# A hybrid decoder layer on one core: the down projection's first right blocks on GpSimd's DMA queue, its last chunk's steps in another order, and the closing squares of the rows ahead of their scalings

## The chip, the cores and the metric

The kernel runs on one core of a Trainium2 chip. Its engines work side by side, each with its own instruction stream: TensorE (PE in the profile, its weight loads PEld) multiplies, VectorE (DVE) does elementwise work on two operands, ScalarE (ACT) does elementwise functions of one operand and row sums of them, GpSimd (POOL) here only issues DMA transfers, among them those that add to what the target holds, and SyncE (SP) only issues plain transfers. An engine waits for another through semaphores, and what stands behind a waiting instruction on the same engine waits with it. The metric is the device time of one execution in microseconds (us), the median of several runs; lower is better.

## The reference

One decoder layer on x of 1024 tokens by 1024 channels, in fp32, cut to what matters here:

```python
h = rms_norm(x, g_mix)
z = h @ w_in + b_in
...                                   # a convolution branch and a recurrent branch, gated and merged
x = x + m @ w_o
h = rms_norm(x, g_mlp)
f = jnp.square(jax.nn.relu(h @ w_1))  # 1024 tokens x 4096
x = x + f @ w_2                       # the down projection: 4096 -> 1024
return rms_norm(x, g_final)
```

`rms_norm(y, g)` is `y * rsqrt(mean(y * y) + EPS) * g`, by rows (tokens). The change touches the last two lines: the down projection `f @ w_2` and the final norm.

## The kernel before

**Arithmetic.** Every fp32 operand of a product is split into a high part (rounded to the matmul's input type fp32r) and a low part, the remainder; high x high, low x high and high x low are summed. A high part is an ACT copy. The remainder is made in one of two ways: by a DVE subtraction (`low`, L1175), or by `split_dma` (L63): ACT writes the negated source as fp32r (L65), a DMA on GpSimd's queue adds the source to it (L66), and ACT writes the high part (L67).

**Down projection.** `f @ w_2` is done by a Winograd form of Strassen's scheme: tokens, inner dimension and output columns are halved, and seven products p = 1 to 7 take the place of eight. The inner dimension is cut into four chunks g = 0 to 3 (`NC_`), and a product has two halves kk in each; so a chunk has 14 steps m = 0 to 13, of 24 matmuls each. Steps run p = 1, 2, 6, 5, 7, 3, 4, in the last chunk 1, 2, 6, 5, 3, 7, 4. Within a step two halves of the tokens q2 = 0, 1 are two groups of 12 matmuls.

**Names in the trace.** `fd` is the DRAM buffer with f's blocks, written by `up_first` (from tiles `fa`, L1717) and `up_second` (from `fb`, L1709). `ar` and `br` are raw left blocks (from `fd`) and right blocks (from `w_2`), loaded by `d_load` (L1820). `s` and `t` are their sums and differences (`d_sum`, L1829; `t1`, `t3`, `t4`, `s3`, `s4` overwrite a raw block). `da_60h` and `da_60l` are the high and low left operand of p = 6, kk = 0 in any chunk, `db_...` the right one; the text writes `da3_60l` where the chunk matters. `d0a`, `d0b`, `d0e` are the PSUM units of chunk 0, each of 1024 columns, from a pool of four. `acc` are the four output quadrants in SBUF; `xb` are blocks of the residual that start or join them (`x_block`, L1975).

**What a step does.** `left_high` (L1867) makes the next step's left operand, `right` (L1875) the right operand of the step after that. `right` takes `split_dma` for p = 1 in chunk 0; for kk = 0 and for p = 2 and 5 in the other chunks; and the DVE subtraction otherwise. `down_mm` issues the matmuls, `down_add` (L1962) copies p = 1's result to the unit `b` (ACT, L1966), so that p = 2 can go on in unit `a`, and adds the other results to `acc` (DVE, L1970). `SUMS` and `LAST` say in which step each of the sums is made, `XADD` when a residual block is added.

**Entry.** The up projection runs before, in the same written order. Its last steps call `entry(k)`, k steps before the end: the loads of chunk 0 (all on SP's queue), and the first operands (`right(0, 1, 0)`, `left_high(0, 1, 0)`, `right(0, 1, 1)`). `DLOADS` lists the blocks by the step of the chunk before in which they are loaded for the other chunks; `DFIRST`, two more left blocks, follow in step 0 of their own chunk.

**End.** In the last chunk `FX` adds work to the steps: squares of finished rows with their row sums (`out_sq`), products with the final gain (`out_pre`), root and scaling of the first four row tiles (`out_root`, `out_scaled`), and operands of p = 4 and 7 by `by_dma`. The product p = 4 comes last and apart: `d_last` (L2032) puts unit `b` plus the accumulator into PSUM units `f`, and four groups of 12 matmuls add p = 4 to f0 to f3, one row tile of 128 tokens each. f0 and f1 are the halves of one PSUM unit; f2 and f3 have one each. `close(n)` (L2045) then finishes row tile 4 + n: square and row sum of `f` (ACT, L2050), root (ACT, L2051), reciprocal with a Newton step (DVE, L98 to L105), scaling of both column halves (DVE, L2056 and L2058; for the last two tiles ACT, L2055), and the transfer to the output.

**Order.** ACT, DVE and PE run in the order in which the code issues (`manual_schedule`); the order on SP's and POOL's queues is the scheduler's. Pools of SBUF tiles are rings: a load waits until the tile that had its place is no longer read. Tiles of one pool hold `fa`, `fb` and the operands `da`, `db`; another holds raw blocks, sums and the rows of the output. The last lines of the code before:

```python
d_group(du["f", 0], z, 4, 0, (0, 1), False, True)
d_last(1)
out_root(1)
out_sq(1, 1, 0)
out_scaled(1)
out_sq(1, 1, 1)
out_pre(1, 1, 1)
d_group(du["f", 1], z, 4, P, (0, 1), False, True)
close(0)
d_group(du["f", 2], z, 4, 2 * P, (0, 1), False, True)
close(1)
d_group(du["f", 3], z, 4, 3 * P, (0, 1), False, True)
close(2)
close(3)
```

Of the kernel before, what the change touches and what calls it, by code (L numbers as in the profile page):

```python
# [12 lines left out]
AF = mybir.ActivationFunctionType  # L13
ALU = mybir.AluOpType
# [3 lines left out]
D = 1024  # L18
# [6 lines left out]
EPS = 1e-6  # L25
# [5 lines left out]
def trunk_kernel(ctx: ExitStack, tc: tile.TileContext, x, xt_in, xt_eo, vecs, w_in, w_a_out, w_b_pl, w_b_sq,  # L31
                 w_rg, w_o, w_1, w_2, g_final, out):

    nc = tc.nc
# [19 lines left out]
    HALVES = (slice(0, HS), slice(HS, S))  # L54
# [729 lines left out]
    for i in range(2, NZ):  # L784
        n = zseq.index((i, 1))
# [18 lines left out]
    with tc.manual_schedule(engines=ENGINES):  # L804
        for s in range(3, NC1):
# [45 lines left out]
            for d in range(5):  # L851
                if s - d in EXP:
                    g = EXP[s - d]
# [6 lines left out]
                    t = 3 * g + d - (2 if g < 3 else 1)  # L860
# [119 lines left out]
    with tc.manual_schedule(engines=ENGINES):  # L980
# [72 lines left out]
        sb, yb_, fs = {}, {}, {}  # L1053
# [86 lines left out]
        for n in range(len(zseq) + 2):  # L1140
# [9 lines left out]
            if n + 3 < len(zseq):  # L1150
                i, p = zseq[n + 3]
# [26 lines left out]
    q, mean, vacc, rstd, nsum, nspl = {}, {}, {}, {}, {}, {}  # L1178
# [131 lines left out]
    m, sa, x1 = {}, {}, {}  # L1310
# [501 lines left out]
    NC_ = NP // KC  # L1812
# [7 lines left out]
    def d_load(g, *what):  # L1820
        for side, b, kk in what:
            n = 2 * g + kk
            ab[side, g, kk, b] = a = T(f"{side}r{n}_{b}")
            if side == "a":
                nc.sync.dma_start(v3(a), fd[2 * n:2 * n + 2, :, BLK[b], :].rearrange("k p c -> p k c"))
            else:
                nc.sync.dma_start(a, w_2[n, b // 10 - 1, b % 10 - 1])

    def d_sum(g, kk, name):  # L1829
        n = 2 * g + kk  # L1830
# [42 lines left out]
        split_dma(*d_pair(side, g, p, kk))  # L1873

    def right(g, p, kk):  # L1875
        if (p == 1 if g == 0 else not kk or p in (2, 5)):
            by_dma("b", g, p, kk)
            return lambda: None
        src, h, l = d_pair("b", g, p, kk)
        nc.scalar.activation(h, src, AF.Copy)  # L1880
        return lambda: low(l, src, h)
# [5 lines left out]
    DFIRST = ("a", 22, 1), ("a", 12, 1)  # L1887

    def entry(k):
        if k == 10:  # L1890
            for n in range(5, 9):
                d_load(0, *DLOADS[n])
        elif k == 7:
            d_load(0, *DLOADS[9])
        elif k == 6:
            d_load(0, *DLOADS[10], DLOADS[11][0])
        elif k == 5:
            d_load(0, DLOADS[11][1], *DLOADS[12])
            right(0, 1, 0)
        elif k == 4:  # L1900
            left_high(0, 1, 0)()
            d_load(0, *DLOADS[13])
        elif k == 3:
            right(0, 1, 1)

    ready = 4
    with tc.manual_schedule(engines={mybir.EngineType.Activation, mybir.EngineType.DVE,
                                     mybir.EngineType.PE}):
        for n in range(len(useq)):
# [4 lines left out]
            while ready < min(len(useq), n + look + 1):  # L1914
                i, p = useq[ready]
# [23 lines left out]
    du = {}  # L1939
# [4 lines left out]
    def d_group(o, g, p, c0, kks, start, stop):  # L1944
        todo = []
        for kk in kks:
            (ah, al), (b_h, b_l) = ([v3(a) for a in opn[side, g, p, kk]] for side in "ab")
            c = slice(c0, c0 + P)
            todo += [x for k in range(2) for x in ((ah[:, k, c], b_h[:, k, :]), (al[:, k, c], b_h[:, k, :]))]
            todo += [(ah[:, k, c], b_l[:, k, :]) for k in range(2)]  # L1950
        for n, (a, b) in enumerate(todo):
            nc.tensor.matmul(o, a, b, start=start and n == 0, stop=stop and n == len(todo) - 1,  # L1952
                             skip_group_check=not start or not stop)
# [29 lines left out]
    dseq = [(g, p, kk) for g in range(NC_) for p in (DORD if g < NC_ - 1 else (1, 2, 6, 5, 3, 7, 4))  # L1983
            for kk in range(2)]
    SUMS = {0: ("t1",), 1: ("t2", "s1"), 2: ("s2",), 4: ("t3",), 5: ("s3",), 7: ("s4",), 9: ("t4",)}
    LAST = {0: ("t1",), 1: ("t2", "s1"), 2: ("s2",), 4: ("s4",), 6: ("t3",), 7: ("s3",), 8: ("t4",)}
    XADD = {(0, 5): (0, 1, 0), (0, 7): (0, 1, 1), (1, 3): (1, 0, 0), (1, 7): (1, 0, 1),
            (2, 3): (1, 1, 0), (2, 7): (1, 1, 1)}

# [4 lines left out]
    gfin = outt = None  # L1994
    sts, ro = {}, {}
# [12 lines left out]
    def out_pre(r, c, q2):  # L2008
        for q in range(2):
            tt(ro[tok(r, q2, q)][:, HALVES[c]], acc[r, c, q2][:, HALVES[q]], gfin[:, HALVES[c]], ALU.mult)  # L2010

    def out_root(q2):
        v, s = (sts[0, q2][:, i] for i in (2, 3))
        tt(v, sts[0, q2][:, 0], sts[0, q2][:, 1], ALU.add)
        nc.vector.tensor_scalar(v, v, 1.0 / D, EPS, ALU.mult, ALU.add)
        nc.scalar.activation(s, v, AF.Sqrt)
# [4 lines left out]
    def out_scaled(q2):  # L2021
        v, s, u, r = (sts[0, q2][:, i] for i in (2, 3, 4, 5))
        newton_rstd(r, v, s, u, False)
        for q in range(2):
            t = tok(0, q2, q)
            lo, hi = HALVES
            nc.scalar.activation(ro[t][:, lo], ro[t][:, lo], AF.Copy, scale=r[:, q:q + 1])
            nc.vector.scalar_tensor_tensor(ro[t][:, hi], acc[0, 1, q2][:, HALVES[q]], r[:, q:q + 1], gfin[:, hi],
                                           ALU.mult, ALU.mult)
            nc.sync.dma_start(rows(t), ro[t])  # L2030
# [12 lines left out]
        down_add(NC_ - 1, 7, q2)  # L2043

    def close(n):  # L2045
        t, (lo, hi) = 4 + n, HALVES
        ps, (q2, q) = du["f", n], divmod(n, 2)
        sa, sb, v, s, u, r = (sts[1, q2][:, i, q:q + 1] for i in range(6))
        nc.vector.tensor_scalar(sb, sb, 1.0 / D, EPS, ALU.mult, ALU.add)
        nc.scalar.activation(ro[t][:, lo], ps, AF.Square, accum_out=sa)  # L2050
        nc.scalar.activation(s, sa, AF.Sqrt, scale=1.0 / D, bias=sb)  # L2051
        nc.vector.scalar_tensor_tensor(v, sa, 1.0 / D, sb, ALU.mult, ALU.add)
        newton_rstd(r, v, s, u, root=False)
        if q2:
            nc.scalar.activation(ro[t][:, hi], ro[t][:, hi], AF.Copy, scale=r)  # L2055
        nc.vector.scalar_tensor_tensor(ro[t][:, lo], ps, r, gfin[:, lo], ALU.mult, ALU.mult)  # L2056
        if not q2:
            nc.vector.scalar_tensor_tensor(ro[t][:, hi], acc[1, 1, 0][:, HALVES[q]], r, gfin[:, hi],  # L2058
                                           ALU.mult, ALU.mult)
        if n < 3:  # L2060
            nc.sync.dma_start(rows(t), ro[t])
        else:
            nc.sync.dma_start(rows(t)[:, lo], ro[t][:, lo])
            nc.scalar.dma_start(rows(t)[:, hi], ro[t][:, hi])

    def last_begun():
# [3 lines left out]
        for r in range(2):  # L2070
# [1 line left out]
                sts[r, q2] = cp.tile([P, 6, 2], F32, tag="stl", name=f"st_last{r}{q2}", bufs=4)  # L2072

    z = NC_ - 1
    FX = {2: ((last_begun,),), 4: ((out_sq, 0, 0, 0),), 5: ((out_sq, 0, 0, 1), (out_pre, 0, 0, 0)), 7: ((out_pre, 0, 0, 1),),
          9: ((by_dma, "a", z, 7, 1), (by_dma, "b", z, 4, 0), (by_dma, "a", z, 4, 0), (out_sq, 0, 1, 0)),
          10: ((by_dma, "b", z, 4, 1), (by_dma, "a", z, 4, 1), (out_root, 0), (out_sq, 0, 1, 1), (out_scaled, 0))}
    held, xbs = None, {}
    with tc.manual_schedule(engines={mybir.EngineType.Activation, mybir.EngineType.DVE,
                                     mybir.EngineType.PE}):  # L2080
        for n, (g, p, kk) in enumerate(dseq[:-2]):
            m = n % 14
            end = g == NC_ - 1
            nx, nx2 = dseq[n + 1], dseq[n + 2]
            if m in DLOADS and not end:
                d_load(g + 1, *DLOADS[m])
            elif m == 0:
                d_load(g, *DFIRST)
            if n == 0:
                for q2 in range(2):  # L2090
                    acc[0, 0, q2] = x_block(0, 0, q2)
            if (g, m) in XADD:
                xbs[g, m] = x_block(*XADD[g, m])
            if held:
                held.pop()()
            lows_ = []
            if not end or m < 10:
                lows_.append(left_high(*nx))
            sums_ = d_sums(g, m)
            if sums_:  # L2100
                d_sum(*sums_.pop(0))
            if not end or m < 10:
                lows_.append(right(*nx2))
            down_mm(g, p, kk, 0)
            if kk:
                if end and p == 7:
                    d_last(0)
                else:
                    down_add(g, p, 0)
            for f in lows_:  # L2110
                f()
            for x in sums_:
                d_sum(*x)
            if (g, m - 4) in XADD:
                k = XADD[g, m - 4]
                tt(acc[k], acc[k], xbs.pop((g, m - 4)), ALU.add)
            down_mm(g, p, kk, 1)
            if kk:
                held = [lambda g=g, p=p: down_add(g, p, 1)]
            if end:  # L2120
                for f, *a in FX.get(m, ()):
                    f(*a)
        d_group(du["f", 0], z, 4, 0, (0, 1), False, True)
        d_last(1)
        out_root(1)
        out_sq(1, 1, 0)
        out_scaled(1)
        out_sq(1, 1, 1)
        out_pre(1, 1, 1)
        d_group(du["f", 1], z, 4, P, (0, 1), False, True)  # L2130
        close(0)
        d_group(du["f", 2], z, 4, 2 * P, (0, 1), False, True)
        close(1)
        d_group(du["f", 3], z, 4, 3 * P, (0, 1), False, True)
        close(2)
        close(3)


def layout(i):
# [72 lines left out]
```

## Time and profile before

| | |
|---|---|
| median of 3 runs | 1540.06 us (1539.85 to 1541.54) |
| the profiled execution | 1541.44 us, its span 1539.6 us |
| mean granted clock of TensorE | 0.998 |
| transferred | 304.16 MB, mean 198 GB/s |

The profile is one execution, recorded on the chip. Times in it are us from the start of the span; a row of a timeline gives the start, the duration, the engine, the line of the code, the operation, output and inputs (without their numbers), and, in brackets, the idle time of the engine before it with what ended it. The chain that ended last is followed back from the last instruction to whatever released each. A row on transfers gives the number, the size of one and the median time from issue to landing; a row on a queue gives packets, MB and the time of the packets as a share of 16 engines. Matmuls overlap: one of 0.39 us is followed by the next 0.23 us later.

### The profile page before, as it was taken

How to read it: one execution, taken by the hardware profiler on the slowest of the kernel's cores; microseconds unless marked ns; L12 is line 12 of the kernel's file. 1: busy time of each engine (PE TensorE's matmuls, PEld its weight loads, DVE VectorE, ACT ScalarE, POOL GpSimd, SP SyncE). 2: the span in 40 equal slices, each digit the busy share in tenths (PEclk: the TensorE clock that was granted, in tenths of full speed). 3: DMA queues.
4: the chain of work that ended last, by engine and by line, in shares of the span. 5: the costliest groups of instructions: out<-in, count | busy, mean ns of one | idle time of the engine just before them, and what ended most of it. 6: DMA issues, size and time to landing. Idle time of an engine off the chain costs nothing.

```text
span 1539.6 us, 19032 instructions
## 1 busy us (share of the span) xinstructions
PE 1523.6 (99%) x6734; PEld 1253.0 (81%) x6734; DVE 1218.0 (79%) x1647; ACT 909.9 (59%) x1272; POOL 169.2 (11%) x204
## 2 busy tenths in 40 slices
PE   9999999999999999999999999999999999999997
PEld 7888888888888888888888888888888888888875
DVE  6899999979899998788868879755555387777676
ACT  6648576657667566645575777544444454545465
POOL 0000000002222222000022322000000000101011
PEclk9999999999999999999999999999999999999999
DMA  8776978898998789963779898333333965767346
GB/s 347 197 190 158 251 188 217 220 264 226 245 254 204 193 192 249 309 225 121 268 198 304 180 209 199 133 135 111 111 110 116 318 222 137 197 172 206 67 83 178
DMA packets 132433, 304.16 MB, mean 198 GB/s; under 512 B 13248, under 2 KB 35264, under 8 KB 132336
## 3 DMA queue, kind: packets, MB, share of 16 engines
q1 hardware_dynamic: 104048, 234.79, 46.2%
q0 software_dynamic: 28144, 67.88, 24.1%
q8 instruction: 53, 0.87, 0.2%
q14 instruction: 44, 0.36, 0.1%
q10 hardware_dynamic: 144, 0.26, 0.0%
HBM read 149.79 MB, written 60.82 MB: 137 GB/s over the span
## 4 chain that ended last, share of the span: by engine, by line
PE 89%; issue 5%; DMA 3%; DVE 2%; POOL 1%; ACT 1%; SPq 0%; POOLq 0%; DVEq 0%; ACTq 0%
PE z L726 15%; PE d0b L1952 2%; PE d2b L1952 2%; PE d1b L1952 2%; PE z L258 2%; PE d0e L1952 1%; PE d3b L1952 1%; PE d3a L1952 1%; PE d2e L1952 1%; PE d2a L1952 1%; PE d1e L1952 1%; PE d1a L1952 1%; PE d3e L1952 1%; DMA win_raw<-in_w_in_dram 1%; PE rg L534 1%
## 5 line engine op out<-in xcount | busy, mean ns | idle before, releaser
L726 PE MATMUL z<-xh,win_h 128*128 128x512 f32 x400 | 124.9, 390 | 0.0
L726 PE MATMUL z<-xl,win_h 128*128 128x512 f32 x400 | 124.5, 389 | 0.0
L726 PE MATMUL z<-xh,win_l 128*128 128x512 f32 x400 | 98.4, 391 | 0.6 <-DMA win_l<-win_raw 0.6
L726 PEld LDWEIGHTS z<-xh,win_l 128*128 128x128 f32 x400 | 75.0, 188 | 17.9 <-DMA win_l<-win_raw 1.1
L726 PEld LDWEIGHTS z<-xh,win_h 128*128 128x128 f32 x400 | 75.0, 188 | 16.8 <-ACT win_h L67 0.7
L637 DVE SCALAR_TENSOR_TENSOR y<-u,vec,y 128x511 f32<-128x511 f32 (+14 forms) x120 | 88.3, 736 | 0.0
L726 PEld LDWEIGHTS z<-xl,win_h 128*128 128x128 f32 x400 | 75.1, 188 | 15.8
L542 ACT ACTIVATE g<-rg,vec 96x1024 f32<-96x1024 f32 x32 | 35.6, 1113 | 85.7 <-issue 46.0
L637 DVE SCALAR_TENSOR_TENSOR yt<-u,vec,yt 128x511 f32<-128x511 f32 (+6 forms) x112 | 82.5, 737 | 0.0
L637 DVE SCALAR_TENSOR_TENSOR y<-yt,csum,y 128x511 f32<-128x511 f32 (+6 forms) x112 | 82.5, 737 | 0.0
L1648 ACT ACTIVATE o<-s 128x512 fp32r<-128x512 f32 x56 | 33.7, 623 | 45.7 <-DVE s L1632 26.4
L66 POOL DMA_DIRECT2D win_l<-win_raw x25 | 21.5, 859 | 325.8 <-ACT win_l L65 313.5
L486 DVE SCALAR_TENSOR_TENSOR v<-xb,vec,v 128x1023 f32<-128x1023 f32 (+2 forms) x36 | 46.2, 1283 | 7.0 <-ACT v L477 6.1
L66 POOL DMA_DIRECT2D zo<-zw x42 | 36.2, 861 | 128.5 <-ACT zo L65 111.9
L66 POOL DMA_DIRECT2D db_10l<-br x4 | 3.4, 860 | 340.1 <-DMA br<-in_w_dram 254.1
L65 ACT ACTIVATE zo<-zw 128x512 fp32r<-128x512 f32 x42 | 26.3, 626 | 20.7 <-PE z9f L914 2.1
L1176 DVE TENSOR_TENSOR o<-s,o 128x512 fp32r<-128x512 f32 x56 | 37.3, 683 | 1.4 <-ACT o L1648 1.4
L66 POOL DMA_DIRECT2D zo<-zs x28 | 24.2, 863 | 77.2 <-ACT zo L65 71.9
L578 DVE TENSOR_TENSOR_SCAN g<-a,g 128x1024 f32<-128x1024 f32 x12 | 27.5, 2292 | 0.4
L67 ACT ACTIVATE win_h<-win_raw 128x1024 fp32r<-128x1024 f32 x25 | 26.1, 1046 | 0.0
L65 ACT ACTIVATE win_l<-win_raw 128x1024 fp32r<-128x1024 f32 x25 | 26.1, 1045 | 0.0
L67 ACT ACTIVATE zo<-zw 128x512 fp32r<-128x512 f32 x42 | 26.1, 621 | 0.0
(3122 smaller groups left out, 4829.9 us busy)
## 6 DMA issues: line engine op xcount, KB each, us to landing
w_raw<-in_w_dram SPq DMA_DIRECT2D x34, 512.0 KB, 5.5
br<-in_w_dram SPq DMA_DIRECT2D x32, 512.0 KB, 5.9
ar<-fd SPq DMA_DIRECT2D x32, 512.0 KB, 6.6
zw<-in_w_in_dram SPq DMA_DIRECT2D x28, 512.0 KB, 6.4
win_raw<-in_w_in_dram SPq DMA_DIRECT2D x25, 512.0 KB, 6.6
win_l<-win_raw POOLq DMA_DIRECT2D x25, 512.0 KB, 7.2
zo<-zw POOLq DMA_DIRECT2D x42, 256.0 KB, 5.7
gates<-zg SPq DMA_DIRECT2D x32, 256.0 KB, 4.1
```

The lines of the kernel that those rows point to most:

```text
L65: nc.scalar.activation(l, src, AF.Copy, scale=-1.0)
L66: nc.gpsimd.dma_start(l, src, accum_op=ALU.add)
L67: nc.scalar.activation(h, src, AF.Copy)
L258: nc.tensor.matmul(z0[i][:, HALVES[hf]], w0[i][w][:, k, :], xpart(a, hf, k), start=k == 0 and which == "hh", stop=k == 7 and which == ("hl ...
L486: nc.vector.scalar_tensor_tensor(v[:, d:S], a[:, 0:S - d], cbw_c[:, w * 12 + t:w * 12 + t + 1], v[:, d:S], ALU.mult, ALU.add)
L542: nc.scalar.activation(a, gps.pop((n, gi))[:HD, :], AF.Sigmoid, bias=(ba_c, bx_c)[gi][:, n:n + 1])
L578: nc.vector.tensor_tensor_scan(i, a, i, 0.0, ALU.mult, ALU.add)
L637: nc.vector.scalar_tensor_tensor(o[:, k:], a[:, 0:HS - k], c, o[:, k:], ALU.mult, add)
L726: nc.tensor.matmul(zps[s][:, HALVES[hf]], w[:, k, :], xw[k][part][hf], start=n == 0, stop=n == 23)
L1176: tt(l, src, h.bitcast(F32), ALU.subtract)
L1648: nc.scalar.activation(o[:, 0], src, AF.Copy)
L1952: nc.tensor.matmul(o, a, b, start=start and n == 0, stop=stop and n == len(todo) - 1, skip_group_check=not start or not stop)
```

## The change

It has four parts.

- Loads: chunk 0's right blocks are loaded by GpSimd's queue, the others still by SP's; `entry` starts them earlier or in other steps, and `DFIRST` of chunk 0 moves from step 0 to `entry(4)`.
- `right`: p = 2 takes `split_dma` in every chunk, so `db0_20` and `db0_21` change over from the subtraction; so does `db3_31`.
- Last chunk: `t3` is made two steps earlier and `s3` one step earlier (`LAST`), and `FX` is reordered; `out_root(1)` and `out_scaled(1)` move from behind `d_last(1)` into step 10.
- `close` is cut in two: `close(n)` has the square, its row sum and the root, `closed(n)` the reciprocal, the scalings and the transfers. `close(0)` stands ahead of f1's group, `close(1)` ahead of f2's, `close(2)` ahead of f3's; `closed(2)` and `closed(3)` come last.

```diff
             else:
-                nc.sync.dma_start(a, w_2[n, b // 10 - 1, b % 10 - 1])
+                (nc.sync if g else nc.gpsimd).dma_start(a, w_2[n, b // 10 - 1, b % 10 - 1])
...
     def right(g, p, kk):
-        if (p == 1 if g == 0 else not kk or p in (2, 5)):
+        if p == 2 or (p == 1 if g == 0 else not kk or p == 5 or (g, p) == (NC_ - 1, 3)):
             by_dma("b", g, p, kk)
             return lambda: None
...
     def entry(k):
-        if k == 10:
+        if k == 12:
             for n in range(5, 9):
                 d_load(0, *DLOADS[n])
+        elif k == 8:
+            d_load(0, *DLOADS[9])
         elif k == 7:
-            d_load(0, *DLOADS[9])
+            d_load(0, *DLOADS[10])
         elif k == 6:
-            d_load(0, *DLOADS[10], DLOADS[11][0])
+            d_load(0, *DLOADS[11])
         elif k == 5:
-            d_load(0, DLOADS[11][1], *DLOADS[12])
+            d_load(0, *DLOADS[12])
             right(0, 1, 0)
         elif k == 4:
             left_high(0, 1, 0)()
-            d_load(0, *DLOADS[13])
+            d_load(0, *DLOADS[13], *DFIRST)
...
-    LAST = {0: ("t1",), 1: ("t2", "s1"), 2: ("s2",), 4: ("s4",), 6: ("t3",), 7: ("s3",), 8: ("t4",)}
+    LAST = {0: ("t1",), 1: ("t2", "s1"), 2: ("s2",), 4: ("s4", "t3"), 6: ("s3",), 8: ("t4",)}
...
     def close(n):
+        t, lo = 4 + n, HALVES[0]
+        sa, sb, s = (sts[1, n // 2][:, i, n % 2:n % 2 + 1] for i in (0, 1, 3))
+        nc.vector.tensor_scalar(sb, sb, 1.0 / D, EPS, ALU.mult, ALU.add)
+        nc.scalar.activation(ro[t][:, lo], du["f", n], AF.Square, accum_out=sa)
+        nc.scalar.activation(s, sa, AF.Sqrt, scale=1.0 / D, bias=sb)
+
+    def closed(n):
         t, (lo, hi) = 4 + n, HALVES
-        ps, (q2, q) = du["f", n], divmod(n, 2)
+        q2, q = divmod(n, 2)
         sa, sb, v, s, u, r = (sts[1, q2][:, i, q:q + 1] for i in range(6))
-        nc.vector.tensor_scalar(sb, sb, 1.0 / D, EPS, ALU.mult, ALU.add)
-        nc.scalar.activation(ro[t][:, lo], ps, AF.Square, accum_out=sa)
-        nc.scalar.activation(s, sa, AF.Sqrt, scale=1.0 / D, bias=sb)
         nc.vector.scalar_tensor_tensor(v, sa, 1.0 / D, sb, ALU.mult, ALU.add)
...
-    FX = {2: ((last_begun,),), 4: ((out_sq, 0, 0, 0),), 5: ((out_sq, 0, 0, 1), (out_pre, 0, 0, 0)), 7: ((out_pre, 0, 0, 1),),
-          9: ((by_dma, "a", z, 7, 1), (by_dma, "b", z, 4, 0), (by_dma, "a", z, 4, 0), (out_sq, 0, 1, 0)),
-          10: ((by_dma, "b", z, 4, 1), (by_dma, "a", z, 4, 1), (out_root, 0), (out_sq, 0, 1, 1), (out_scaled, 0))}
+    FX = {2: ((last_begun,),), 4: ((out_sq, 0, 0, 0),), 5: ((by_dma, "a", z, 4, 0), (out_sq, 0, 0, 1)),
+          6: ((by_dma, "a", z, 4, 1), (out_pre, 0, 0, 1)), 8: ((by_dma, "a", z, 7, 1), (out_pre, 0, 0, 0)),
+          9: ((by_dma, "b", z, 4, 0), (out_sq, 0, 1, 0), (out_root, 0)),
+          10: ((by_dma, "b", z, 4, 1), (out_sq, 0, 1, 1), (out_scaled, 0), (out_root, 1), (out_scaled, 1))}
...
-            elif m == 0:
+            elif m == 0 and g:
                 d_load(g, *DFIRST)
...
         d_group(du["f", 0], z, 4, 0, (0, 1), False, True)
         d_last(1)
-        out_root(1)
         out_sq(1, 1, 0)
-        out_scaled(1)
         out_sq(1, 1, 1)
         out_pre(1, 1, 1)
+        close(0)
         d_group(du["f", 1], z, 4, P, (0, 1), False, True)
-        close(0)
+        closed(0)
+        close(1)
         d_group(du["f", 2], z, 4, 2 * P, (0, 1), False, True)
-        close(1)
+        closed(1)
+        close(2)
         d_group(du["f", 3], z, 4, 3 * P, (0, 1), False, True)
-        close(2)
         close(3)
+        closed(2)
+        closed(3)
```

More of the change, by code (lines that the diff above doesn't have):

```diff
@@ L2055, in close @@
             nc.scalar.activation(ro[t][:, hi], ro[t][:, hi], AF.Copy, scale=r)
-        nc.vector.scalar_tensor_tensor(ro[t][:, lo], ps, r, gfin[:, lo], ALU.mult, ALU.mult)
+        nc.vector.scalar_tensor_tensor(ro[t][:, lo], du["f", n], r, gfin[:, lo], ALU.mult, ALU.mult)
         if not q2:
```

## The prediction

> **What bounds the kernel now.** I read the page first, then the engines' timelines through the down projection, then the transfers and the queues around its first chunk. The first fence is the page: span, busy time of TensorE, the chain by engine.
>
> ```profile
> span 1539.6 us, 19032 instructions
> PE 1523.6 (99%) x6734; PEld 1253.0 (81%) x6734; DVE 1218.0 (79%) x1647; ACT 909.9 (59%) x1272; POOL 169.2 (11%) x204
> PE 89%; issue 5%; DMA 3%; DVE 2%; POOL 1%; ACT 1%; SPq 0%; POOLq 0%; DVEq 0%; ACTq 0%
> ```
>
> TensorE (PE) is busy 99%, and the change removes no matmul. So it can be worth only the gaps of PE in the last fifth of the span, plus what runs after the last matmul. The sum is made against the profiled span of 1539.6 and carried over to the median of the runs, 1540.06; the profiled execution took 1541.44, 1.84 more than its span and 1.38 over the median. A run cannot tell less than 0.2%, 3.1 us, from no change.
>
> PE's timeline (start, duration, operation, releaser) at chunk 0 of the down projection:
>
> ```profile
> 1231.71 0.39 PE L1952 MATMUL d0a<-db_20h,da_20h 128*128 128x512 f32 x1
> ...
> 1237.15 0.39 PE L1952 MATMUL d0a<-db_21h,da_21h 128*128 128x512 f32 x1
> ...
> 1238.06 0.62 PE L1952 MATMUL d0a<-db_21l,da_21h 128*128 128x512 f32 x2
> ...
> 1242.59 0.39 PE L1952 MATMUL d0b<-db_60h,da_60h 128*128 128x512 f32 x1
> 1243.78 0.50 PE L1952 MATMUL d0b<-db_60h,da_60l 128*128 128x512 f32 x1 [0.80 <-DVE da_60l L1176]
> ...
> 1249.15 0.39 PE L1952 MATMUL d0b<-db_61h,da_61h 128*128 128x512 f32 x1
> ```
>
> An undisturbed step takes 1242.59 - 1237.15 = 5.44. The step from 1242.59 took 6.56: **1.12 lost in chunk 0**, waiting for a remainder (the low operand) that VectorE (DVE) subtracts. The same view of chunk 3:
>
> ```profile
> 1494.05 0.39 PE L1952 MATMUL d3e<-db_30h,da_30h 128*128 128x512 f32 x1
> ...
> 1498.55 0.50 PE L1952 MATMUL d3e<-db_30h,da_30h 128*128 128x512 f32 x1 [1.62 <-DVE acc L1970]
> ...
> 1501.41 0.39 PE L1952 MATMUL d3e<-db_31h,da_31h 128*128 128x512 f32 x1
> ```
>
> This step took 7.36: **1.92 lost in chunk 3**, waiting until DVE has added a product's sum. I found no other stall of PE in the four chunks. The end, by timelines of PE, ACT, DVE, and one piece of the chain (the x4 row):
>
> ```profile
> 1517.73 0.39 PE L1952 MATMUL f<-db_40h,da_40h 128*128 128x512 f32 x1
> 1520.45 0.39 PE L1952 MATMUL f<-db_40h,da_40h 128*128 128x512 f32 x1
> 1528.16 0.61 PE L1952 MATMUL f<-db_41l,da_41h 128*128 128x512 f32 x2
> 1519.14 1.21 DVE L1970 TENSOR_TENSOR acc<-acc,d3b 128x1024 f32<-128x1024 f32 x1
> 1520.86 1.23 ACT out L2005 x4
> 1532.73 0.58 ACT L2050 ACTIVATE out<-f 128x512 f32<-128x512 f32 x1
> 1534.59 0.75 DVE L2056 SCALAR_TENSOR_TENSOR out<-f,st_last,gfin 128x512 f32<-128x512 f32 x1
> 1535.34 0.40 ACTq L2064 DMA_DIRECT2D out_dram<-out  x1
> ```
>
> PE is done at 1528.77; the four closings of rows then run one behind another, and the last scaling starts 5.82 later.
>
> **Chunk 3's sums.** DVE around the stall:
>
> ```profile
> 1492.66 1.22 DVE L1176 TENSOR_TENSOR da_30l<-ar,da_30h 128x1024 fp32r<-128x1024 f32 x1
> ...
> 1497.28 1.21 DVE L1970 TENSOR_TENSOR acc<-acc,d3e 128x1024 f32<-128x1024 f32 x1
> ```
>
> Between the two run one remainder, one sum and two output products (3.4 us). The new order puts none of them there: db3_31's remainder goes by DMA, the sum and `out_pre` move. The add then ends near 1495.4. PE needs it one group of matmuls (1520.45 - 1517.73 = 2.72) after 1494.05, at 1496.77. So all of the stall goes: **-1.92**. What moves to steps 5 to 10 seems to fit, the first low operand of p=7 most tightly. Bounds -1.92 to 0.
>
> **The end.** In the changed order ACT runs both squares of `out_sq(1,1,1)`, then the square of f0; and the first matmul of f1 waits for that square, since f0 and f1 are halves of one PSUM tile. Before, nothing read f0 before f1 had run. With PE 1.92 earlier, DVE's last add ends at 1520.35 - 1.92 = 1518.43, two squares with their reads take 1.23, f0's square 0.58 and some 0.1 of hand-over: 1520.35. Unstalled, f1 would start at 1518.53. So a **new stall of 1.9** takes chunk 3's gain back (0 if the wait isn't in force; 2.1 if hand-overs are slower), and f3 ends near 1528.77 as before.
>
> Behind f3 the chain is now short, as closings 0 to 2 have their squares ahead. From the square of f3 to its scaling it took 1534.59 - 1532.73 = 1.86; starting at 1528.9 the scaling starts at 1530.8 instead of 1534.59: **-3.8**. The last two outputs now leave within 1 us of each other; I take 0.3 for that (0 to 1.3): -3.5, with bounds -2.5 to -3.8.
>
> PSUM, in the Trainium skill's "PSUM — Partial Sum Buffer", section "PSUM bank collisions raise a hardware error", is to be guarded by bank, and two 512-column halves of fp32 are two banks. By that rule f1 needn't wait; it is a rival below.
>
> **Chunk 0's operands.** Two remainders (db0_20, db0_21) leave DVE for ACT plus an accumulating DMA on GpSimd's queue. DVE, ACT, then SP's and POOL's queues with issues to landing:
>
> ```profile
> 1231.15 1.23 DVE L1176 TENSOR_TENSOR db_21l<-br,db_21h 128x1024 fp32r<-128x1024 f32 x1 [1.18 <-DMA fd<-fb]
> ...
> 1242.51 1.22 DVE L1176 TENSOR_TENSOR da_60l<-s,da_60h 128x1024 fp32r<-128x1024 f32 x1
> ```
> ```profile
> 1227.65 1.06 ACT L1869 ACTIVATE da_20h<-ar 128x1024 fp32r<-128x1024 f32 x1 [3.74 <-DMA fd<-fa]
> 1228.61 1.04 ACT L1880 ACTIVATE db_21h<-br 128x1024 fp32r<-128x1024 f32 x1
> 1229.56 1.01 ACT L1966 ACTIVATE d0b<-d0a 128x1024 f32<-128x1024 f32 x1
> ```
> ```profile
> 1210.76 2.71 SPq L1978 DMA_DIRECT2D xb<-x1d  x1
> 1220.52 0.33 SPq L1717 DMA_DIRECT2D fd<-fa  x1
> 1220.95 0.46 SPq L1978 DMA_DIRECT2D xb<-x1d  x1
> 1217.43 0.86 POOL L66 DMA_DIRECT2D db_11l<-br  x1 [9.98 <-ACT db_11l L65]
> db_11l<-br POOLq DMA_DIRECT2D x1, 512.0 KB, 7.9
> fd<-fa SPq DMA_DIRECT2D x1, 512.0 KB, 7.0
> xb<-x1d SPq DMA_DIRECT2D x1, 512.0 KB, 15.5
> db_10l<-br POOLq DMA_DIRECT2D x1, 512.0 KB, 10.1
> db_20l<-br POOLq DMA_DIRECT2D x1, 512.0 KB, 4.5
> ```
>
> DVE does two 1.1 us operations less ahead of da_60l, so that remainder is ready some 2 us earlier, and it was 1.12 late: **-1.12**.
>
> What is late next? ACT makes da0_20h only when the store fd<-fa (its buffer) has landed, at 1220.52 + 7.0 = 1227.56; behind it stand db0_21's copy and the copy of d0a that frees the bank for PE's step at 1231.71. That copy ended at 1230.57. The new copy for db0_21l stands ahead of it, 0.96 more, so it ends 3.98 after the landing L: PE stalls from L = 1227.73 on, 0.17 after today's landing.
>
> L moves up for two reasons. The second x block is now ahead of the store on SP's queue: the first landed at 1210.76 + 15.5 = 1226.27, the store 1.3 behind it, so one more in front makes 1228.87. And db0_20l's accumulation now follows db_11l's (landed 1225.37) at once. Two 8 us windows, from 1220 (an accumulation in flight for most of it) and from 1232 (none), give the rates:
>
> ```profile
> q1 hardware_dynamic: 1003, 2.21, 72.7%
> q0 software_dynamic: 144, 0.52, 32.8%
> q1 hardware_dynamic: 1252, 3.13, 103.2%
> ```
>
> SP's queue moved 276 KB/us with and 391 without one in flight. The 3.5 us that were left at 1225.37 become 3.5 x 391/276 = 5.0: L = 1230.3, a stall of **2.6**. Bounds: 0 (landing as before) and 8.3 (the 15.5 that the x block took: L = 1236.0).
>
> By the Trainium skill's "DMA: Bandwidth & Descriptors", section "Queues, rings and completion order", each engine takes turns between queues packet by packet; equal halves of 391 would give L near 1232.4, an estimate, and the sum 2.1 more. The trace's 1003 packets to 144 look kinder, though db_11l wasn't in flight throughout.
>
> db0_21l is issued 2.2 after L and needed at 1238.06 plus the stall. With T from issue to landing, both waits together are the larger of L - 1227.73 and L + T - 1235.86. T lies between 4.5 (idle transfers) and 15.5; under load 7.9 and 10.1 were seen, so I take 9.0: 3.4 together, **0.9** more than the first wait.
>
> GpSimd's queue for the eight `br` blocks costs nothing here: POOL was idle for 254 us before db_10l, as its row shows,
>
> ```profile
> 1206.59 0.86 POOL L66 DMA_DIRECT2D db_10l<-br  x1 [254.05 <-DMA br<-in_w_dram]
> ```
>
> the loads wait for the same buffers, and db_10l, now queued behind them, landed at 1216.65, over 4 us ahead of chunk 0 (which starts two steps before 1231.71, at 1220.83). Without that slack each microsecond would count in full (bounds 0 to +1.3, a landing's spacing). I expect no gain from it either.
>
> **Sum.** -1.12 + 2.6 + 0.9 (chunk 0) - 1.92 + 1.9 - 3.5 = -1.2, so 1540.06 - 1.2 = 1538.9.
>
> **Rivals.**
> - Transfers have room: the store lands by 1227.73 and db0_21l in time. For: DMA engines weren't full while accumulations ran. Against: the extra x block ahead. -1.12 - 3.5 = -4.6: 1535.4.
> - f1 doesn't wait for f0's square: another -1.9, so -3.1: 1537.0. For: nothing but the banks; against: the instruction order has the wait.
> - Slower: the store takes the x block's 15.5 behind the fuller ring. Both waits then are 8.3 to 10.2, the sum +3.7 to +5.6: 1543.7 to 1545.7. It decides from 7.7 together, which is L beyond 1235.4, or L = 1230.3 with T over 13.3. For: 15.5 was reached 10 us earlier; against: only two accumulations are in flight.
> - The change doesn't do what it says: chunk 3's stall only moves to another operand (p=7's), while f1 waits as reckoned: -1.2 + 1.92 = +0.7, 1540.8; with the outputs at 1.3 instead of 0.3 and T at 10.1 it is +2.8, 1542.9, and a little more in hand-overs passes 0.2%. For: DVE and ACT are in a fixed order there with much moved; against: db3_31's remainder leaves DVE.
>
> **How the numbers follow.** Forecast 0.44, its own range 1537.1 to 1541 (sums -3 to +1). Room 0.28. No wait 0.05. Slower store 0.17. Stall only moved 0.06, half of it over 0.2%. Faster by over 0.2% is the first two rivals, 0.33; slower 0.17 + 0.03 = 0.20; within 0.2% 0.44 + 0.03 = 0.47. The range of 8 in 10 takes in the room case and part of the slow ones: 1534.9 to 1542.7.
>
> **What would show it.** Chunk 0: PE waits at the first db_20 matmul for ACT's copy of d0a, then perhaps at db_21l for GpSimd's DMA, and no longer at da_60l. Chunk 3: no wait for DVE's add. End: PE waits about 1.9 before f1 for an ACT square, and the last scaling starts 2 us behind the last matmul, not 5.8. It is wrong if chunk 0 runs without a wait, if f1 follows f0 at once, or if a stall appears where I named none.

## The result and the profile after

The changed kernel takes 1543.79 us (median of 13 runs, 1542.58 to 1545.71) against 1540.21 before (13 runs beside them): 1.0022 times the time before, 95% interval 1.0013 to 1.0030. It is slower by 3.6 us, where 1.2 us less was forecast, and lies 1.1 us above the stated range. The profiled execution is the slowest of the 13, 1545.71 us with a span of 1543.9.

The first rows are the page of the changed kernel: span, busy times, the chain by engine.

```profile
span 1543.9 us, 19040 instructions
PE 1525.3 (99%) x6734; PEld 1254.0 (81%) x6734; DVE 1214.3 (79%) x1644; ACT 912.9 (59%) x1275; POOL 178.1 (12%) x215
PE 92%; DMA 3%; issue 2%; DVE 1%; ACT 1%; POOL 1%; SPq 0%; POOLq 0%; DVEq 0%; ACTq 0%
```

PE has the same 6734 matmuls, yet is busy 1.7 us longer: some of them ran slower. The next rows are PE's timeline at chunk 0, at the place where the bank of d0a must be free.

```profile
1226.81 0.39 PE L1954 MATMUL d0a<-db_11h,da_11h 128*128 128x512 f32 x1
...
1231.80 0.61 PE L1954 MATMUL d0a<-db_11l,da_11h 128*128 128x512 f32 x2
1238.01 0.80 PE L1954 MATMUL d0a<-db_20h,da_20h 128*128 128x512 f32 x1 [5.60 <-ACT d0b L1968]
1238.60 0.63 PE L1954 MATMUL d0a<-db_20h,da_20l 128*128 128x512 f32 x1
...
1246.40 0.39 PE L1954 MATMUL d0a<-db_21h,da_21h 128*128 128x512 f32 x1
```

The first row starts the second step of p = 1, and the second row ends it. p = 2 would have started at 1232.25, one step of 5.44 behind 1226.81; it started at 1238.01, so 5.76 were lost. The step that follows took 8.39 instead of 5.44: another **2.95**, as matmuls in its first part lasted 0.63 instead of 0.39. The table of windows (length; busy time and count of PE, PEld, DVE, ACT, POOL; granted clock of TensorE; DMA share; GB/s) shows why:

```profile
1220.00:1228.00 8.00, 8.00 (x37) 6.62 (x36) 3.68 (x5) 4.93 (x6) 0.86 (x1) 1.00 1.06 309
...
1236.00:1244.00 8.00, 5.99 (x14) 4.75 (x15) 7.95 (x8) 4.78 (x6) 0.86 (x1) 0.58 1.01 316
```

The granted clock is 0.58 in the second window, which begins 2 us before the wait ends; from 1238 to 1244 alone it is 0.50. What PE waited for is in the timelines of ACT and of SP's queue, with a row on the store's transfer:

```profile
1223.91 1.06 ACT L1708 ACTIVATE fb<-fb 128x1024 f32<-128x1024 f32 x1
1234.10 1.06 ACT L1869 ACTIVATE da_20h<-ar 128x1024 fp32r<-128x1024 f32 x1 [9.13 <-DMA fd<-fa]
1235.06 1.04 ACT L65 ACTIVATE db_21l<-br 128x1024 fp32r<-128x1024 f32 x1
1236.01 1.04 ACT L67 ACTIVATE db_21h<-br 128x1024 fp32r<-128x1024 f32 x1
1236.95 1.91 ACT L1968 ACTIVATE d0b<-d0a 128x1024 f32<-128x1024 f32 x2
```
```profile
1209.86 6.64 SPq L1980 DMA_DIRECT2D xb<-x1d  x2
1221.06 0.33 SPq L1717 DMA_DIRECT2D fd<-fa  x1
fd<-fa SPq DMA_DIRECT2D x1, 512.0 KB, 13.0
```

The store took 13.0 from issue to landing instead of 7.0, ACT stood for 9.13 us, and PE went on 3.95 behind the landing (1221.06 + 13.0 = 1234.06), where 3.98 was reckoned. The other two places, again on PE's timeline, with ACT's square of f0 and DVE's last scaling:

```profile
1502.19 0.39 PE L1954 MATMUL d3e<-db_30h,da_30h 128*128 128x512 f32 x1
...
1507.63 0.39 PE L1954 MATMUL d3e<-db_31h,da_31h 128*128 128x512 f32 x1
```
```profile
1523.95 0.39 PE L1954 MATMUL f<-db_40h,da_40h 128*128 128x512 f32 x1
1527.85 0.57 ACT L2051 ACTIVATE out<-f 128x512 f32<-128x512 f32 x1
1528.56 0.50 PE L1954 MATMUL f<-db_40h,da_40h 128*128 128x512 f32 x1 [1.73 <-ACT out L2051]
1536.41 0.61 PE L1954 MATMUL f<-db_41l,da_41h 128*128 128x512 f32 x2
1538.94 0.75 DVE L2062 SCALAR_TENSOR_TENSOR out<-f,st_last,gfin 128x512 f32<-128x512 f32 x1
```

Chunk 3's step takes 5.44 again: its 1.92 are gone. f1 starts 1.89 later than one group behind f0 (1523.95 + 2.72). The last scaling starts 1.92 behind the last matmul (1537.02) instead of 5.82.

The two profiles differ by 4.3 in span: 0.54 by which this execution was late already at chunk 0's start (a scatter of single executions), + 5.76 + 2.95 - 1.12 in chunk 0, - 1.92 in chunk 3, + 1.89 at f1, - 3.90 at the closings, and some 0.1 that I didn't place.

### The profile page after: what moved, and what is told of

Read it like the earlier page. It is cut to its first block, busy times and chain, and to the rows that moved or that the text cites. A ratio compares the mean times of both kernels' runs of the same rounds, so it can differ in the third digit from the quotient of the medians.

```text
span 1543.9 us, 19040 instructions
## 1 busy us (share of the span) xinstructions
PE 1525.3 (99%) x6734; PEld 1254.0 (81%) x6734; DVE 1214.3 (79%) x1644; ACT 912.9 (59%) x1275; POOL 178.1 (12%) x215
## 4 chain that ended last, share of the span: by engine, by line
PE 92%; DMA 3%; issue 2%; DVE 1%; ACT 1%; POOL 1%; SPq 0%; POOLq 0%; DVEq 0%; ACTq 0%
PE z L726 18%; PE d2b L1954 2%; PE d1b L1954 2%; PE d0b L1954 2%; PE d0e L1954 1%; PE d3b L1954 1%; PE d3e L1954 1%; PE d3a L1954 1%; PE d2e L1954 1%; PE d2a L1954 1%; PE d1e L1954 1%; PE d1a L1954 1%; PE z L258 1%; PE rg L534 1%; PE rg L536 1%
## 5 line engine op out<-in xcount | busy, mean ns | idle before, releaser
L1827 POOL DMA_DIRECT2D br<-in_w_dram x8 | 4.2, 532 | 249.7 <-DVE o L1176 238.4
```

## The experiments

All compare with the kernel before, run beside them. The question was what makes the store late, whether its landing alone makes the wait, and what the end is worth.

**Subtractions back on VectorE** in chunk 0:

```diff
-        if p == 2 or (p == 1 if g == 0 else not kk or p == 5 or (g, p) == (NC_ - 1, 3)):
+        if (p == 1 if g == 0 else not kk or p in (2, 5) or (g, p) == (NC_ - 1, 3)):
```

> The changed kernel with db0_20 and db0_21 back to VectorE's subtraction. Theory (the accumulations): db0_20l's accumulation slows SyncE's queue while the store fd<-fa of the last block waits in it, and db0_21l's copy stands ahead of the copy that frees PE's bank. Without both the store lands at 1229 to 1231 instead of 1234.0, PE waits 0 to 2 us at the first db_20 matmul instead of 5.6, runs at full clock behind it, and VectorE's own loss of 1.1 comes back: 1535.5 to 1538.5. Rival (the loads): blocks on GpSimd's queue and the x block ahead of the store are what delays it; then the wait stays over 3.5 us with slow matmuls behind it: 1541 to 1543.

Measured: 1538.61 us, 0.9988 times before (0.9979 to 0.9998). PE's timeline and the store:

```profile
1232.89 0.50 PE L1954 MATMUL d0a<-db_20h,da_20h 128*128 128x512 f32 x1 [2.00 <-ACT d0b L1968]
fd<-fa SPq DMA_DIRECT2D x1, 512.0 KB, 10.3
```

The wait fell to 2.00 and no slow stretch followed (0.14 in the step); da_60l's wait is back in part (0.78 in its step). The wait lies at the upper bound that the theory allowed, and the time 0.1 above it. But the store still took 10.3: the accumulation explains 2.7 of the 6.0 us by which it is late, not all. The rival has a share.

**Right blocks back on SyncE's queue**, which puts the second x block behind the store too:

```diff
-                (nc.sync if g else nc.gpsimd).dma_start(a, w_2[n, b // 10 - 1, b % 10 - 1])
+                nc.sync.dma_start(a, w_2[n, b // 10 - 1, b % 10 - 1])
```

> The changed kernel with chunk 0's right blocks on SyncE's queue, which also puts the second x block behind the store fd<-fa again. Theory (the accumulations): the store gains at most the x block's 1.3 us, the wait stays over 3 us: 1540.5 to 1543. Rival (the loads): the store lands within 9 us of its issue, PE waits under 1.5 us: 1535 to 1538.

Measured: 1540.35 us, 0.9999 (0.9990 to 1.0009), between the two expectations. PE's two waits in chunk 0, and the store:

```profile
1232.76 0.50 PE L1954 MATMUL d0a<-db_20h,da_20h 128*128 128x512 f32 x1 [2.32 <-ACT d0b L1968]
...
1240.41 0.72 PE L1954 MATMUL d0a<-db_21l,da_21h 128*128 128x512 f32 x2 [1.00 <-DMA db_21l<-br]
fd<-fa SPq DMA_DIRECT2D x1, 512.0 KB, 9.7
```

Queue and x block together are worth 3.3 us of the store's landing. Here db_21l's accumulation is late as well, as the prediction had it for a shorter first wait. The profiled execution, 1539.43 us, is the second quickest of the ten, so others may have lost more than these rows show.

**The second x block behind the store**, all else as changed:

```diff
-            if n == 0:
-                for q2 in range(2):
-                    acc[0, 0, q2] = x_block(0, 0, q2)
+            if n in (0, 2):
+                acc[0, 0, n // 2] = x_block(0, 0, n // 2)
```

> The changed kernel with the second x block loaded two steps later, behind the store fd<-fa on SyncE's queue; nothing else moves on that queue. If the x block's place is a main cause, the store lands 1.3 to 2.6 us earlier and the wait and its slow matmuls shrink: 1539 to 1541.5. If the accumulations or GpSimd's loads are, less than 1 us: 1543 to 1544.

Measured: 1541.16 us, 1.0004 (0.9994 to 1.0013), so the first expectation.

```profile
1234.54 0.80 PE L1954 MATMUL d0a<-db_20h,da_20h 128*128 128x512 f32 x1 [3.62 <-ACT d0b L1968]
fd<-fa SPq DMA_DIRECT2D x1, 512.0 KB, 11.0
```

The x block's place is worth 2.0 of the store's landing. The wait is 3.62 in PE's row (3.78 in the step), and the step behind it is still 2.88 too long. The runs go from 1539.42 to 1542.55, the widest of all versions: with a wait of this length a slow stretch may follow or not, which I take for the cause of the spread, but as only one execution was profiled, that isn't shown.

**Only the last chunk and the closings changed**, chunk 0 as before: the first two edits above, the old `entry`, and

```diff
-            elif m == 0 and g:
+            elif m == 0:
                 d_load(g, *DFIRST)
```

> The changed kernel with the whole of chunk 0 as before (loads, their steps, subtractions); only the last chunk and the closings are changed. By every theory chunk 0 then loses 1.1 as before, chunk 3's 1.9 is gone, f1 waits 1.9, and the last scaling starts 1.9 instead of 5.8 behind the last matmul: 1540.2 - 3.9 = 1536.3, 1535.8 to 1537. Over 1538 would mean that the end isn't worth what the trace of the changed kernel shows.

Measured: 1537.19 us, 0.9980 (0.9971 to 0.9990), 0.2 above the expected bounds.

```profile
1243.12 0.50 PE L1952 MATMUL d0b<-db_60h,da_60l 128*128 128x512 f32 x1 [1.06 <-DVE da_60l L1176]
fd<-fa SPq DMA_DIRECT2D x1, 512.0 KB, 7.0
```

The last chunk and the end gain 3.3 by themselves; the old wait at da_60l is there (1.39 in its step), and the store lands in 7.0 again. By this version and the changed kernel, chunk 0's part of the change costs 1543.79 - 1537.19 = 6.6.

**Own buffers.** da0_20 and db0_21 take tiles from the ring of raw blocks, so that ACT needn't wait for the store; all transfers stay:

```diff
-        mk = d_home(g, p)
+        mk = T if (side, g, p, kk) in (("a", 0, 2, 0), ("b", 0, 2, 1)) else d_home(g, p)
```

> The changed kernel with the four tiles of da0_20 and db0_21 in the ring of raw blocks instead of the ring that fa and the operands share; every load, accumulation and instruction stays. ScalarE then no longer waits for the store fd<-fa before da0_20. Theory (the store's landing, through this buffer, makes chunk 0's wait; the transfers as such hurt nobody): the 5.8 us wait and the 2.9 us of slow matmuls behind it go though the store still lands 12 to 13 us after its issue: 1543.8 - 8.7 = 1535.1, up to 1536.5 if db0_21l's accumulation is a little late. Rival (the crowded queues would stall PE on other operands as well): another wait of 3 us or more in chunk 0, 1538 to 1542.

Measured: 1536.05 us, 0.9972 (0.9963 to 0.9981), within the theory's bounds. ACT's timeline and the store:

```profile
1222.63 1.05 ACT L1869 ACTIVATE da_20h<-ar 128x1024 fp32r<-128x1024 f32 x1
...
1228.58 1.01 ACT L1968 ACTIVATE d0b<-d0a 128x1024 f32<-128x1024 f32 x1 [2.06 <-PE d0a L1954]
...
1233.98 1.06 ACT L1869 ACTIVATE da_21h<-ar 128x1024 fp32r<-128x1024 f32 x1 [1.68 <-DMA fd<-fa]
fd<-fa SPq DMA_DIRECT2D x1, 512.0 KB, 14.0
```

The store takes 14.0, longer than ever, and PE doesn't wait at p = 2: the copy of d0a comes when PE is done with it. The edit moves four tiles, but in the changed kernel only da_20h's copy stood waiting, for the store, and the three copies behind it followed at once. So it is through this wait that the crowded queues cost PE its 8.7 us. What is late next is small: da_21h now waits for the store, and da_60l, behind it on DVE, held PE for 0.8 in this profile.

**f1 ahead of close(0)**, on the version with chunk 0 as before:

```diff
-        close(0)
         d_group(du["f", 1], z, 4, P, (0, 1), False, True)
+        close(0)
         closed(0)
         close(1)
```

> The changed kernel with chunk 0 as before, and with close(0) behind f1's group instead of ahead of it. Theory (f1 waits for f0's square because both are in one PSUM unit): the wait of 1.9 at f1 goes, and as the closings of f0 and f1 run beside f2 and f3 nothing is late behind it: 1.9 less than with close(0) ahead, 1537.2 - 1.9 = 1535.3. Rival (VectorE's closings then set the end): under 0.7 of it shows, 1536.5 to 1537.2.

Measured: 1536.14 us, 0.9972 (0.9961 to 0.9982), 1.05 less than with close(0) ahead: between the expectations. The traces are nearer to the second one: from f0's first matmul to the last scaling it is 15.00 us with close(0) ahead and 14.61 with f1 first, 0.39 less; what the rest of the 1.05 is, they don't show. **Both edits together:**

> The changed kernel with both edits: own buffers for da0_20 and db0_21, and close(0) behind f1's group. If both theories hold the gains add: 1535.1 - 1.9 = 1533.2, 1532.8 to 1534.6, faster than either kernel. If chunk 0 waits elsewhere or VectorE sets the end, 1535 or more.

Measured: 1535.11 us, 0.9966 (0.9954 to 0.9979), so the second expectation. The last matmul and the last scaling of this version:

```profile
1525.00 0.61 PE L1954 MATMUL f<-db_41l,da_41h 128*128 128x512 f32 x2
1529.18 0.75 DVE L2062 SCALAR_TENSOR_TENSOR out<-f,st_last,gfin 128x512 f32<-128x512 f32 x1
```

f1 waits no more, but the scaling starts 3.57 behind the last matmul instead of 1.92: with PE 1.9 earlier, VectorE's closings, one behind another, set the end and take most of it back. To relieve VectorE there, the upper halves of the first two closings go the way of the last two, and close(1) stands ahead of closed(0):

```diff
-        if q2:
-            nc.scalar.activation(ro[t][:, hi], ro[t][:, hi], AF.Copy, scale=r)
+        nc.scalar.activation(ro[t][:, hi], ro[t][:, hi], AF.Copy, scale=r)
...
-        if not q2:
-            nc.vector.scalar_tensor_tensor(ro[t][:, hi], acc[1, 1, 0][:, HALVES[q]], r, gfin[:, hi],
-                                           ALU.mult, ALU.mult)
...
+        out_pre(1, 1, 0)
         out_pre(1, 1, 1)
         d_group(du["f", 1], z, 4, P, (0, 1), False, True)
         close(0)
-        closed(0)
         close(1)
+        closed(0)
```

> The version with own buffers and f1 first, with VectorE relieved at the end: the upper column halves of the first two closings are multiplied by the gain earlier (out_pre) and scaled by ScalarE, as in the last two, and close(1) stands ahead of closed(0). Theory (with f1 first, VectorE's chain of closings sets the end, the last scaling 3.6 us behind the last matmul instead of 1.9): it starts 1.9 to 2.2 behind it, 1535.1 - 1.5 = 1533.6. Rival (the wait of ScalarE's second square for VectorE's scaling of f0 sets it, and something else takes its place): over 1534.6.

Measured: 1534.49 us (five runs, 1533.12 to 1535.44), 0.9960 (0.9946 to 0.9974): the best version, 6 us under the kernel before.

```profile
1523.78 0.61 PE L1954 MATMUL f<-db_41l,da_41h 128*128 128x512 f32 x2
1526.56 0.75 DVE L2061 SCALAR_TENSOR_TENSOR out<-f,st_last,gfin 128x512 f32<-128x512 f32 x1
```

The scaling starts 2.17 behind the last matmul, as expected. The time is 0.6 under the version before it, not 1.5; the runs scatter by more than that, so the trace shows the gain and the times don't settle its size.

**A long wait**, in the version with f1 ahead and chunk 0 as before: the copy of d0a is done 13 times.

```diff
-            nc.scalar.activation(du["b", q2], ps, AF.Copy)
+            for _ in range(13 if (g, q2) == (0, 0) else 1):
+                nc.scalar.activation(du["b", q2], ps, AF.Copy)
```

> The version of close(0) behind f1's group with chunk 0 as before, and with the copy of d0a that frees PE's bank done 13 times over, so that PE waits some 10 us at the first db_20 matmul. Theory (a wait over some 3 us costs a fixed stretch of slow matmuls behind it, as after waits of 3.8 and 5.8 us): 2.9 us again behind it. Rival (the longer the wait, the longer the slow stretch): 5 us or more.

Measured: 1548.11 us in one run.

```profile
1242.03 0.80 PE L1952 MATMUL d0a<-db_20h,da_20h 128*128 128x512 f32 x1 [11.32 <-ACT d0b L1967]
1242.62 0.63 PE L1952 MATMUL d0a<-db_20h,da_20l 128*128 128x512 f32 x1
...
1245.79 0.39 PE L1952 MATMUL d0a<-db_20h,da_20l 128*128 128x512 f32 x1
```

After a wait of 11.3 the matmuls were slow until 1245.6 and the step cost 1.75 more, less than after 3.6 or 5.6. So neither expectation held in this one run: the stretch doesn't grow with the wait, and it isn't a fixed 2.9 either.

## Why the prediction was wrong

The step that failed is chunk 0's. It was forecast to lose 2.4 (-1.12 + 2.6 + 0.9), and by the profiles it lost 7.6 (5.76 + 2.95 - 1.12): the store's landing was mis-sized, and the slow matmuls behind a longer wait had no term. Chunk 3 and the end came to -3.9, where the sum had -3.5. (The sum's terms add up to -1.1, it says -1.2; those of f1's stall give 1.82, it says 1.9. Neither matters here.)

- **Chunk 3's sums, right.** -1.92 forecast and measured.
- **f1's wait, right.** 1.9 forecast, 1.89 measured, for ACT's square as named; the rival by which f1 doesn't wait did not come. That it needn't exist is shown by the version with f1 first; what it hides is VectorE's closings, which I hadn't seen as the next thing late.
- **Closings, right.** -3.8 forecast, -3.9 measured; the 0.3 for the last outputs wasn't there: from the last scaling's start to the end of the span it is 4.96 after and 5.01 before. Without chunk 0's part the end and chunk 3 gained 3.3 in the times, where the sum had -1.92 + 1.9 - 3.5 = -3.5.
- **da_60l, right for this kernel**: it has no wait there. With own buffers, where PE comes to p = 6 without the 8.7 us of loss, one profile shows the wait again (0.80), and the two versions after it lose 0.00 and 0.03 in that step. So the gain isn't safe.
- **Chunk 0's store: the mechanism right, the term mis-sized.** "L = 1230.3, a stall of 2.6": from its issue that is 9.8; it took 13.0. My sum had 1.3 for the x block, 1.4 for the accumulation, nothing for the loads on GpSimd's queue. The runs show, one edit at a time, 2.0 for the x block (13.0 to 11.0), 1.3 for GpSimd's queue (11.0 to 9.7), and 2.7 for the accumulations (13.0 to 10.3; and again 9.7 to 7.0, where the steps of `entry` went back as well), which add up to the 6.0. Each is from one profiled execution. The 6.0 is firm, as the four versions with chunk 0 as before have 7.0 to 7.2. The shares are less so: the three versions with own buffers, whose transfers are the changed kernel's with db0_21l's earlier, have 14.0, 12.6 and 12.9. The accumulation was sized by a mean over 8 us, 276 against 391; the last section shows that it moves its data in 3 us and takes some 2.5 us (an estimate) from SP's queue at once. "GpSimd's queue for the eight `br` blocks costs nothing here" was wrong: I looked at who waits for these loads and not at what they take from the queue beside them; how they delay the store isn't shown. By the Trainium skill's "DMA: Bandwidth & Descriptors", section "Queues, rings and completion order", with its turns between queues, L would have been 1232.4, an estimate; that is 11.9 from the issue, nearer to the 13.0 than my 9.8. The trace agrees with the turns: while an accumulation moved its data, GpSimd's queue had 130 packets and SP's 141. My "1003 packets to 144" counted 8 us, in most of which none moved.
- **The second wait, wrong but small.** 0.9 for db0_21l: with the longer first wait it landed in time.
- **What no term held: slow matmuls behind a wait.** 2.95 of the 8.7 lost in chunk 0. The two waits in the profile before, 0.80 and 1.62, are followed by almost none of it, so that I priced a wait at its length. From 2.3 (0.15 in the step) to 3.6 (2.88) this changes; the 2.6 that I forecast lies between, where no run was made. With the 2.95 the time falls into the range of the rival of the slow store (1543.7 to 1545.7), but not by its sum: the store took 13.0 and not 15.5, and the waits came to 5.76 and not to 8.3 or more. That the time fits its range is luck.

That the landing of this one store is the cause is shown by the version with own buffers, which keeps every transfer, lets the store land as late as ever, and loses neither the 5.76 nor the 2.95.

## What to carry to other kernels

Before adding transfers near a tight hand-over, ask which buffer there is freed by a transfer's landing, and count everything that is now in flight or queued ahead of it, in other queues too; here four tiles that come from another ring were worth 7.7 us. Price a wait of the matrix engine by its length only while it is short: here one of 2.3 us cost 0.15 more, and those of 3.6 us and longer cost 1.8 to 2.9 more, at lower clock. Don't size what an accumulating transfer takes from another queue by a mean over a window in which it mostly didn't move. When a wait is removed from the end of a kernel, look at the engine whose work it covered.

## What the runs showed of the hardware that was not expected

**The clock behind a wait.** Waits of PE and what the next step cost beyond 5.44: 2.00 and 0.14, 2.32 and 0.15, 3.62 and 2.88, 5.60 and 2.95, 11.32 and 1.75. Slow matmuls follow each other at 0.43 us instead of 0.23, and the slow stretches last 6.0, 6.1 and 3.5 us. The Trainium skill's "TensorE: Matmul & The Clock Gate", section "What's actually happening", says that the array's clock is halved after an idle window of about 3.4 us and given back after a busy one, and that the windows run freely. The rows agree on both sides of 3.4 us. Freely running windows would also let the stretch differ from case to case, as 2.9 and 1.75 do; no run here shows the windows themselves.

**Accumulating transfers.** The rate that all transfers reach together falls for a part of the time in which an accumulation between SBUF tiles is in flight. This is the changed kernel's view of transfers from 1220 to 1228 in 40 slices of 0.2 us; db_11l was in flight until 1226.0 and db_20l from 1222.3 on:

```profile
GB/s 410 410 389 430 389 430 389 410 358 399 451 276 236 256 236 256 236 256 236 256 236 256 236 256 236 256 185 328 430 389 430 389 440 92 399 92 379 113 348 154
```

It is about 400 at first, about 245 for 3 us in the middle, and alternates between 400 and 100 at the end, though transfers were waiting on SP's queue throughout. The version with the subtractions back in chunk 0 has no db_20l. Its chunk 0 starts 1.5 earlier, so that 1218.5 to 1226.5 is the same stretch:

```profile
GB/s 430 389 420 389 430 389 399 399 369 389 461 266 246 246 246 246 246 246 246 246 246 246 246 246 246 246 174 369 389 420 399 420 399 389 420 399 420 399 420 430
```

The 3 us in the middle, behind which db_11l lands, are there; the drop at the end is not. So the drops go with the accumulations. These are the packets, MB and shares of 16 engines of the two queues in the changed kernel from 1222.2 to 1225.4:

```profile
q0 software_dynamic: 130, 0.50, 78.8%
q1 hardware_dynamic: 141, 0.28, 25.7%
```

The queues had nearly as many packets each, but GpSimd's, which add to what the target holds, took three times the engines' time. SP's queue moved 0.28 MB in these 3.2 us. At 400 KB/us it needs 0.7 us for that, so one accumulation takes some 2.5 us from it, an estimate from these rows; the store landed 2.7 later with db_20l than without.
